# Four PSUM tiles in turn in place of three kept ones, and another order where pool mixer and output projection meet

## The chip, the cores and the metric

The kernel runs on one core of one Trainium2 chip. The number that counts is the device time in microseconds from the launch to the end of the last instruction; the median of three runs of the kernel before is 1367.88 us (1367.1 to 1373.0). The profiled execution, from which all rows below come, took 1365.11 us, with a span of 1363.2 us from its first to its last instruction. The five engines of the core are named PE (matrix multiply, with PEld for its weight loads), DVE (vector), ACT (scalar), POOL and SP; DMA queues move data between HBM and on-chip memory. Matrix products land in PSUM, which has eight banks of 512 fp32 numbers per partition; DVE or ACT must read a product out of its bank before PE may write there again.

## The reference

The program is one step of a streaming encoder for 1024 new frames of one stream and 32 of another (1056 columns of 1024 channels, all fp32), through two layers.

```
even:  h = rms_norm(x);  z = h @ w_in            # 5120 columns: a | u v | gate
       y_a = pool_mixer(a)                        # trailing means over 2/4/8/16 frames minus a, per-group 256x256 matrix, scale
       y_b = u * (W_s @ layer_norm(v) + b)        # per chunk of 128 frames, gelu(u), gelu(v); 4 head groups ("SGU")
       x = x + rms_norm((concat(y_a, y_b) * silu(gate)) @ w_out)
odd:   z = rms_norm(x) @ w_in                     # q latent | kv latent | rotary key | gate
       attention over latents, chunk-causal;  x = x + rms_norm((out * silu(gate)) @ w_o)
```

Outputs are both streams, the pool mixer's last 15 rows, v of the small stream and the caches of the odd layer.

## The kernel before

**Layout.** Channels lie on the partitions in blocks of 128, frames along the free axis. The 1056 frames are cut into an "a" group of 640 columns and a "b" group of 416. A product of fp32 accuracy is made of three matmuls, hi\*hi, hi\*lo and lo\*hi, on operands that have been split in two; the code names the halves `hi`/`lo`, `whi`/`wlo`. An output block of 128 channels over 8 input blocks takes, for the a group, 24 groups of two matmuls of 320 columns in a two-bank tile (`za`), and, for the b group, 24 matmuls of 416 columns in one bank (`zb`). `mm_block` issues them; "ab" interleaves both, "a" or "b" does one. `evac` and its like read the banks out.

**Stages.** In order of time (us from the span's start): the setup and a first part of the input projection; seven-product pairs of blocks (`pair_block`, to about 360); the *pool stage*, which projects the eight `a` blocks, forms the windowed means on DVE and POOL, and multiplies by the group matrices (`y_a`, about 360 to 476); the *junction*, where the last `y_a` and the first two blocks of the output projection meet (to about 510); the *first a loop*, the output projection's first half for m = 2 to 7, over pool channels; the *second a loop* for m = 0 to 7 over SGU channels (about 589 to 660), each followed by the addition to the first half and a running sum of squares (L828 to L832); the *b stage*, the same for the b columns (about 658 to 742, L842 to L860); then the odd layer, whose input projection runs to about 950. The spatial gating (SGU) is done meanwhile, one chunk of 128 frames at a time: four small groups of four matmuls into a bank tagged `mi`, each read by DVE at L764 and L765 into one of three scratch tiles `tm`, `dgh`, `dgl`.

**What sets the order.** PE runs in the order in which Python emits its instructions. A counter `self.now` adds up the cost of each matmul; at the end of each k step `poll` lets one waiting task go whose due time has come. A task yields the delay to its next step from the table `N`: `N["mixq"]` is the delay between the four `mi` groups of a chunk. Tasks can also be driven to an end ahead of their due times, as before `split_a` ("while len(done) < 5"), which needs five finished chunks. The other engines' order is set by the tile framework's scheduler from the dependencies; so are the semaphores, and a dependency holds for a whole tile, whichever part is written.

**PSUM.** The pool `ps` holds three two-bank tiles `zt` (z_9_80, z_10_81, z_11_82 in the rows below) and two one-bank `mi` tiles. After the pairs of blocks `zrot` deals them out: `za` goes in turn to z_10_81 and z_11_82, `zb` in turn to the two halves of z_9_80. In the junction `B2` is that same tile z_9_80, used as the `za` of the last `y_a`, whose `zb` goes to an `mi` bank; later B2 holds the squares of the second a loop. The squares of the b stage go to one of the other two.

`BOTH` names the blocks of the output projection whose first half is done for a and b together ("ab") in the first a loop, and copied out by `put`; the others' b columns get theirs in the b stage.

Of the kernel before, what the change touches and what calls it, by code (L numbers as in the profile page):

```python
# [10 lines left out]
F32 = mybir.dt.float32  # L11
F32R = mybir.dt.float32r
AF = mybir.ActivationFunctionType
ALU = mybir.AluOpType
AX = mybir.AxisListType
ET = mybir.EngineType
PSUM = bass.MemoryType.PSUM
DRAM = bass.MemoryType.DRAM

P = 128  # L20
# [3 lines left out]
NA, NB, CA = 640, 416, 320  # L24
# [7 lines left out]
        "kn e 2": 4.31, "v p 2": 5.302, "kn o 0": 6.344, "qn o 0": 6.796, "v p 3": 7.31, "v p 4": 8.3,  # L32
        "kn o 1": 8.827, "qn o 1": 10.546, "kn o 2": 12.035, "qn o 2": 12.785}

N = {"tp": 5500, "sa": 9000, "sl": 12000, "sb": 6000, "sbk": 2000, "sg": 500, "x": 462, "mix": 10626, "mixq": 1490, "tr": 717, "lead": 9500, "tr0": 11989, "res": 9194, "ra": 2699,
     "rb": 1574, "ha": 8000, "hb": 5000, "kv": 429, "q": 20908, "k": 34682, "kvs": 1773, "qs": 10662, "rest": 1357, "r1": 1608,
     "r2": 1337, "fa": 5400, "tn": 1800, "w0": 2000, "w1": 1552, "f0": 1645, "f1": 626, "fy": 648}
HF = 6
# [2 lines left out]
HT, HQ = 528, 264  # L41
RAW = 3
LO_POOL = ()
BOTH = (2, 3, 4, 5)
A_ORDER = [6, 7, 4, 5, 2, 3, 0, 1]
KS = 5
NV = 1184
# [25 lines left out]
def two(ap):  # L73
    return ap.rearrange("p (c n) -> p c n", c=2)


class Build:
    def __init__(self, ctx, tc, upto, aps):
        self.ctx, self.tc, self.nc = ctx, tc, tc.nc
        self.upto = upto  # L80
        for k, v in aps.items():
            setattr(self, k, v)
        self.uid = 0
        self.now = 0.0
        self.tasks = []
        self.rr = 0
        self.ca, self.nb = CA, NB
        self.banks = {}
        self.reps = {}
        self.zrot = None  # L90

# [32 lines left out]

    def bank(self, tag):

        if self.zrot and tag in ("za", "zb"):
            r = self.zrot[tag == "zb"]  # L130
            r.append(r.pop(0))
            return r[-1]
        tag, bufs = self.banks.get(tag, (tag, 2))
        return self.t(self.ps, [P, 2, 512] if tag in ("za", "sc") else [P, 512], F32, tag, bufs)

# [188 lines left out]
    def even(self):  # L324
        nc = self.nc
# [3 lines left out]
        L, R, ab, halves, evc = self.L, self.R, self.ab, self.halves, self.evc  # L329
# [68 lines left out]
        zt = self.zt  # L398
# [4 lines left out]
        for g in "ab":  # L403
            acc, *sqs = (v[:, mpos[g]] for v in sums)
            z = [(zt[0], None), (zt[1], None)] if g == "a" else [(None, zt[2][:, i, :]) for i in range(2)]
            for k in range(NK):
                x = split_x(g, k)
# [9 lines left out]
        pairs = [(10, 11), (34, 35), (36, 37), (12, 13), (14, 15), (38, 39)] + [(24 + 2 * i, 25 + 2 * i) for i in range(4)]  # L417
# [71 lines left out]
        for g, z in (("a", zz), ("b", z)):  # L489
# [3 lines left out]
            if g == "a":  # L493
                tp = self.spawn(t_prep(), N["tp"])
            for i in range(2):
                ps = (zt[i], None) if g == "a" else (None, zt[2][:, i, :])
# [40 lines left out]
        for p, (b0, b1) in enumerate(pairs):  # L537
# [18 lines left out]
            else:  # L556
                for e in range(2):
                    i = (b0, b1)[e] % 8
# [2 lines left out]
                        nc.vector.tensor_tensor(u, u, g, ALU.mult)  # L561
                        nc.scalar.dma_start(mBd[i], u)
        self.h2 = [(Pair(None, None), Pair(None, None)) for _ in range(NK)]
        zs = [zt[(7 * len(pairs) + i) % 3] for i in range(3)]
        self.zrot = [[zs[0], zs[2]], [zs[1][:, i, :] for i in range(2)]]


        self.shut(self.lb)
# [1 line left out]
        mix = {}  # L570
# [42 lines left out]
        def y_a(g, w, bank=None):  # L613

            wf = w[0]
            for m in range(2):
                c = [slice(k * 256 + m * P, k * 256 + (m + 1) * P) for k in range(2)]
                ps = self.mm_block(lambda k: (wf[0][:, c[k]], wf[1][:, c[k]]), dhl[g], range(2), ps=bank() if bank else None)
                blk = 2 * g + m
                gt, (pool, o) = gate[blk], mslot[blk]  # L620
                hi, lo = mix[blk] = tuple(ab(pool or self.rb, o + e, F32R) for e in range(2))
                nc.vector.scalar_tensor_tensor(two(gt.a), ps[0][:, :, :CA], self.vec(PSC, blk), two(gt.a), ALU.mult, ALU.mult)
                nc.vector.scalar_tensor_tensor(gt.b, ps[1][:, :NB], self.vec(PSC, blk), gt.b, ALU.mult, ALU.mult)
                for q in "ab":
                    nc.scalar.copy(hi.get(q), gt.get(q))  # L625
                    nc.vector.tensor_tensor(lo.get(q), gt.get(q), hi.get(q), ALU.subtract)
            del dhl[g]
            pfree.extend(held.pop(g))

        wp = {}  # L630
        for i, blk in enumerate(A_ORDER):
# [3 lines left out]
            else:  # L635
                wA = self.prep_w(self.i_wout[0, :, :1024])
            ps = self.mm_block(self.wcol(wts.pop(blk)), h, range(NK))
# [4 lines left out]
            a = pool_evac(blk, ps)  # L642
# [18 lines left out]
            if m in BOTH:  # L661
                nc.scalar.copy(yp[m].b, ps[1][:, :NB])  # L662

        part = {}
        for m in range(2):
            if m == 1:
                wA1 = self.prep_w(self.i_wout[1, :, :1024])
            part[m] = self.mm_block(self.wcol(wA if m == 0 else wA1), mix, A_ORDER[:6], "a", last=False)
        B2 = zs[1]
        y_a(pg, wp[pg], lambda: (B2, self.t(self.ps, [P, 512], F32, "mi")))  # L670
        for m in range(2):
            self.mm_block(self.wcol(wA if m == 0 else wA1), mix, A_ORDER[6:], "a", ps=part[m], first=False)
            put(m, part[m])
        wn = {2: self.prep_w(self.i_wout[2, :, :1024])}

# [143 lines left out]
        for m in range(NK):  # L819
            if m < 7:  # L820
                wn = self.prep_w(self.i_wout[m + 1, :, 1024:], lo_on=nc.vector)
            else:
                wA = self.prep_w(self.i_wout[6, :, :1024], lo_on=nc.vector)
            ps = self.mm_block(lambda k: self.wcol(wB)(k - 8), mix, range(8, 16), "a")
            if m < 7:
                wB = wn
            y = yp[m].a
            nc.vector.tensor_tensor(two(y), two(y), ps[0][:, :, :CA], ALU.add)  # L828
            sq = B2[:, :, :CA]
            nc.scalar.activation(two(acc) if m == 0 else sq, two(y), AF.Square)  # L830
            if m:
                nc.vector.tensor_tensor(two(acc), two(acc), sq, ALU.add)  # L832
        self.res = self.spawn(self.residual("a", acc, yp), N["res"])
        while len(done) < 9 or any(mix[8 + k][0].b is None for k in range(NK)):
            self.step(min((t for t in self.tasks if t is not self.res), key=lambda t: t[:2]))
        acc = ab(self.rb, 8, F32, "b").b
        za = self.zrot[0][0]
        order = [6, 7, 0, 1, 2, 3, 4, 5]
        jobs = [(m, c) for m in order for c in ((1,) if m in BOTH else (0, 1))]
        w = wA  # L840
        for j, (m, c) in enumerate(jobs):
            if j + 1 < len(jobs):  # L842
                mm, cc = jobs[j + 1]
                wn = self.prep_w(self.i_wout[mm, :, cc * 1024 : cc * 1024 + 1024], lo_on=nc.vector)
            if c == 0:
                ps = self.mm_block(self.wcol(w), mix, A_ORDER, "b", last=False)
                w = wn
                continue
            ps = None if m in BOTH else ps
            ps = self.mm_block(lambda k: self.wcol(w)(k - 8), mix, range(8, 16), "b", ps=ps, first=ps is None)  # L850
            w = wn
            y = yp[m].b
            if m in BOTH:
                nc.vector.tensor_tensor(y, y, ps[1][:, :NB], ALU.add)  # L854
            else:
                nc.vector.tensor_copy(y, ps[1][:, :NB])  # L856
            sq = za[:, m % 2, :NB]
            nc.scalar.activation(acc if m == order[0] else sq, y, AF.Square)
            if m != order[0]:
                nc.vector.tensor_tensor(acc, acc, sq, ALU.add)  # L860
# [50 lines left out]
    def odd_in(self):  # L911
# [110 lines left out]
        self.shut(self.evc)  # L1022
        self.shut(self.la)
        self.shut(self.ps)
        self.zrot = None


    def attention(self):
# [455 lines left out]
```

## Time and profile before

| what | value |
|---|---|
| median of three runs | 1367.88 us (1367.1 to 1373.0) |
| profiled execution | 1365.11 us, span 1363.2 us |
| busy | PE 1269.6 us (93%), DVE 860.6 (63%), ACT 552.2 (41%), POOL 306.0 (22%) |
| PE busy 360 to 476 | 101.90 of 116 us |
| PE busy 560 to 640 | 70.26 of 80 us |
| PE busy 640 to 750 | 92.77 of 110 us |
| PE busy 800 to 960 | 142.10 of 160 us |
| mean granted TensorE clock | 0.984 |

PE is busy nearly all the time, so what to read is what PE waits for when it is not. A row of the waits reads: the waiting engine, tile and line, the engine, tile and line that it waited for, and the time in all, the number of waits and the longest. In a timeline row stand the start, the length, the instruction, and in brackets the idle time before it with its releaser. All matmuls stand on L116, since one helper issues them: they are told apart by the names of their tiles.

### The profile page before, as it was taken

The page shows a single profiled execution, that of the slowest core. Times are in us where ns is not written, and L with a number is a line of the kernel's source. Part 1 is how long each engine was busy: PE and PEld are TensorE (multiplying, and loading weights), DVE is VectorE, ACT ScalarE, POOL GpSimd, SP SyncE. Part 2 cuts the span into 40 slices and gives each one's busy share as a digit, 9 for nine tenths or more (in the row PEclk, how much of TensorE's full clock was granted, in tenths as well). Part 3 has the DMA queues.
Part 4 walks back from the last instruction along what each step waited for, and adds up shares of the span by engine and source line. Part 5 has one row for each costly group of instructions (what it writes and reads, how often), then busy time and mean ns, then how long its engine had stood idle before and what let it go on. Part 6 is the DMA issues. An engine that isn't in the chain of part 4 may idle for free. (4 is left out here: it accounts for less than half of the span.)

```text
span 1363.2 us, 22025 instructions
## 1 busy us (share of the span) xinstructions
PE 1269.6 (93%) x8488; PEld 1228.1 (90%) x8488; DVE 860.6 (63%) x1613; ACT 552.2 (41%) x1027; POOL 306.0 (22%) x381
## 2 busy tenths in 40 slices
PE   9899999999988899989987989888999999999995
PEld 8899999999988899978886989888899999998994
DVE  7977776767576545698394833531766576665437
ACT  8634333334232222243242323322656565654431
POOL 0200000000232233534002353221322322222410
PEclk9999999999999999999998989989999999999998
DMA  6022223223323152222462332212111111116425
GB/s 218 32 71 87 87 86 112 102 70 105 118 73 117 50 198 86 85 80 76 129 219 82 105 123 91 98 57 87 33 46 52 46 48 50 41 48 196 152 85 193
DMA packets 75159, 130.73 MB, mean 96 GB/s; under 512 B 10448, under 2 KB 33424, under 8 KB 75056
## 3 DMA queue, kind: packets, MB, share of 16 engines
q1 hardware_dynamic: 56576, 101.24, 23.7%
q10 hardware_dynamic: 18480, 28.09, 5.6%
q8 instruction: 67, 1.10, 0.3%
q14 instruction: 36, 0.29, 0.1%
HBM read 97.42 MB, written 31.88 MB: 95 GB/s over the span
## 5 line engine op out<-in xcount | busy, mean ns | idle before, releaser
L116 PE MATMUL z<-l,whi 128*128 128x264 f32 (+2 forms) x2032 | 395.2, 308 | 31.8 <-DVE l L199 15.3
L116 PEld LDWEIGHTS z<-l,whi 128*128 128x128 f32 x2032 | 319.1, 191 | 39.5 <-DVE l L199 16.6
L116 PE MATMUL z<-l,wlo 128*128 128x264 f32 (+2 forms) x1240 | 269.0, 301 | 0.0
L155 ACT CAST whi<-raw 128x512 fp32r<-128x512 f32 (+1 forms) x180 | 108.1, 603 | 352.5 <-PE z L116 221.1
L156 POOL TENSOR_TENSOR wlo<-raw,whi 128x512 fp32r<-128x512 f32 (+2 forms) x122 | 155.6, 1277 | 348.2 <-ACT whi L155 344.0
L116 PEld LDWEIGHTS z<-l,wlo 128*128 128x128 f32 x1240 | 203.5, 191 | 0.3
L116 PE MATMUL z<-r,whi 128*128 128x264 f32 (+2 forms) x696 | 152.8, 307 | 15.6 <-DVE l L854 5.3
L116 PE MATMUL z<-a,whi 128*128 128x320 f32 x704 | 145.2, 312 | 1.5 <-ACT a L625 0.7
L116 PEld LDWEIGHTS z<-r,whi 128*128 128x128 f32 x696 | 114.5, 191 | 19.2 <-issue 4.8
L116 PEld LDWEIGHTS z<-a,whi 128*128 128x128 f32 x704 | 116.1, 188 | 2.9 <-ACT a L625 0.9
L1131 POOL TENSOR_SCALAR p<-p,nm 128x128 f32<-128x128 f32 (+8 forms) x72 | 53.0, 736 | 165.4 <-DVE nm L1130 130.1
L116 PE MATMUL z<-b,whi 128*128 128x416 f32 x240 | 77.4, 361 | 7.8 <-DVE l L856 2.8
L116 PE MATMUL z<-a,wlo 128*128 128x320 f32 x352 | 80.2, 309 | 0.0
L585 POOL MEMSET r<- 128x16 f32 x8 | 0.9, 112 | 310.4 <-PE mi L525 288.4
L448 ACT CAST whi<-r 128x512 fp32r<-128x512 f32 x56 | 34.8, 621 | 86.6 <-PE z L116 80.1
L1129 ACT ACTIVATE p<-sc,nm 128x128 f32<-128x128 f32 (+8 forms) x72 | 50.6, 703 | 44.7 <-DVE nm L1128 32.5
L116 PEld LDWEIGHTS z<-a,wlo 128*128 128x128 f32 x352 | 61.4, 188 | 0.2
L449 DVE TENSOR_TENSOR wlo<-r,whi 128x512 fp32r<-128x512 f32 x56 | 38.4, 686 | 36.0 <-ACT whi L448 35.9
L116 PE MATMUL sc<-a,whi 128*128 128x400 f32 x256 | 57.6, 346 | 0.2 <-ACT p L1129 0.2
L156 DVE TENSOR_TENSOR wlo<-raw,whi 128x512 fp32r<-128x512 f32 x58 | 39.7, 690 | 28.1 <-ACT whi L155 28.1
L1161 DVE TENSOR_TENSOR pl<-pj,ph 128x512 fp32r<-128x512 f32 (+2 forms) x96 | 51.1, 552 | 7.0 <-ACT ph L1160 6.3
L116 PEld LDWEIGHTS z<-b,whi 128*128 128x128 f32 x240 | 45.6, 192 | 10.3 <-ACT l L662 3.2
(305 smaller groups left out, 2634.4 us busy)
## 6 DMA issues: line engine op xcount, KB each, us to landing
raw<-in_w SPq DMA_DIRECT2D x64, 256.0 KB, 2.7
r<-in_w SPq DMA_DIRECT2D x56, 256.0 KB, 2.7
raw<-in_wout SPq DMA_DIRECT2D x56, 256.0 KB, 3.1
mBd<-r ACTq DMA_DIRECT2D x8, 528.0 KB, 2.7
gAd<-r ACTq DMA_DIRECT2D x8, 528.0 KB, 2.7
l<-mBd SPq DMA_DIRECT2D x8, 528.0 KB, 5.7
vd<-r ACTq DMA_DIRECT2D x16, 256.0 KB, 2.3
r<-vd SPq DMA_DIRECT2D x8, 512.0 KB, 3.6
```

The lines of the kernel that those rows point to most:

```text
L116: self.nc.tensor.matmul(out, lhsT, rhs, start=start, stop=stop)
L155: nc.scalar.copy(hi[:, :m], raw[:, :m])
L156: (lo_on or nc.gpsimd).tensor_tensor(lo[:, :m], raw[:, :m], hi[:, :m], ALU.subtract)
L448: nc.scalar.copy(hi, src)
L449: lo_on.tensor_tensor(lo, src, hi, ALU.subtract)
L585: nc.gpsimd.memset(a[:, 0:16], 0.0)
L1129: nc.scalar.activation(pv, view, AF.Exp, bias=nm[:n, 0:1], accum_out=nm[:n, 1:2])
L1131: nc.gpsimd.tensor_scalar(p[:n, :K], p[:n, :K], nm[:n, 2:3], 1.0, ALU.mult, ALU.mult)
L1161: nc.vector.tensor_tensor(lo[:, :nb, off : off + P], tr[:, :nb, :], hi[:, :nb, off : off + P], ALU.subtract)
```

## The change

After the pairs of blocks the pool `ps` is closed, and a pool `psb` with two tiles for each tag is opened in its place: `za` twice (two banks each), `zb` twice, `mi` twice, again eight banks. `zrot` and `B2` go. In the junction the first block of the output projection is done for a and b together over six of eight input blocks, the last `y_a` follows with tiles of its own, then the second block, and then the rest of both. `BOTH` is (0, 3, 4, 5) in place of (2, 3, 4, 5), so that block 0 has its b columns early and block 2 late, and the b stage goes through the blocks in the order 6, 7, 1, 2, 0, 3, 4, 5. The squares of the second a loop are made in two halves of 320 columns in `zb` banks, and those of the b stage in a `za` tile. `N["mixq"]` goes from 1490 to 2600.

```diff
-... "mix": 10626, "mixq": 1490, "tr": 717, ...
+... "mix": 10626, "mixq": 2600, "tr": 717, ...
-BOTH = (2, 3, 4, 5)
+BOTH = (0, 3, 4, 5)
     def bank(self, tag):
-        if self.zrot and tag in ("za", "zb"):
-            r = self.zrot[tag == "zb"]
-            r.append(r.pop(0))
-            return r[-1]
         tag, bufs = self.banks.get(tag, (tag, 2))
         return self.t(self.ps, [P, 2, 512] if tag in ("za", "sc") else [P, 512], F32, tag, bufs)
...
-        zs = [zt[(7 * len(pairs) + i) % 3] for i in range(3)]
-        self.zrot = [[zs[0], zs[2]], [zs[1][:, i, :] for i in range(2)]]
+        self.shut(self.ps)
+        self.ps = self.open("psb", bufs=2, space=PSUM)
...
-        part = {}
-        for m in range(2):
-            if m == 1:
-                wA1 = self.prep_w(self.i_wout[1, :, :1024])
-            part[m] = self.mm_block(self.wcol(wA if m == 0 else wA1), mix, A_ORDER[:6], "a", last=False)
-        B2 = zs[1]
-        y_a(pg, wp[pg], lambda: (B2, self.t(self.ps, [P, 512], F32, "mi")))
-        for m in range(2):
-            self.mm_block(self.wcol(wA if m == 0 else wA1), mix, A_ORDER[6:], "a", ps=part[m], first=False)
+        part = {0: self.mm_block(self.wcol(wA), mix, A_ORDER[:6], "ab", last=False)}
+        wA1 = self.prep_w(self.i_wout[1, :, :1024])
+        y_a(pg, wp[pg])
+        part[1] = self.mm_block(self.wcol(wA1), mix, A_ORDER[:6], "a", last=False)
+        for m, w in ((0, wA), (1, wA1)):
+            self.mm_block(self.wcol(w), mix, A_ORDER[6:], "a" if m else "ab", ps=part[m], first=False)
             put(m, part[m])
...
-            sq = B2[:, :, :CA]
-            nc.scalar.activation(two(acc) if m == 0 else sq, two(y), AF.Square)
-            if m:
-                nc.vector.tensor_tensor(two(acc), two(acc), sq, ALU.add)
+            for c in range(2):
+                yc, ac = two(y)[:, c], two(acc)[:, c]
+                sq = ac if m == 0 else self.bank("zb")[:, :CA]
+                nc.scalar.activation(sq, yc, AF.Square)
+                if m:
+                    nc.vector.tensor_tensor(ac, ac, sq, ALU.add)
...
-        za = self.zrot[0][0]
-        order = [6, 7, 0, 1, 2, 3, 4, 5]
+        order = [6, 7, 1, 2] + list(BOTH)
...
-            sq = za[:, m % 2, :NB]
+            sq = self.bank("za")[:, 0, :NB]
...
-        self.zrot = None
```

PE issues as many matmuls as before. At three places the rows show what moved. In a row stand the position in the engine's order, the line (the changed file is a few lines shorter), the operation, the written tile and the read ones, and the size.

The first place is PE in the pool stage, where one `y_a` block ends and the next begins (`whi` is a group matrix, the `r` are the two halves of the windowed means). Before:

```order
1610 L116 MATMUL z_9_80<-r_419_4211,whi_4225 128x416
1611 L116 MATMUL z_10_81<-r_418_4210,wlo_4226 128x320 x2
1612 L116 MATMUL z_9_80<-r_418_4210,wlo_4226 128x416
1613 L116 MATMUL z_11_82<-r_400_4067,whi_4225 128x320 x2
1614 L116 MATMUL z_9_80<-r_400_4067,whi_4225 128x416
1615 L116 MATMUL z_11_82<-r_401_4068,whi_4225 128x320 x2
```

and in the changed kernel:

```order
1610 L115 MATMUL zb_4331<-r_423_4219,whi_4233 128x416
1611 L115 MATMUL za_4330<-r_422_4218,wlo_4234 128x320 x2
1612 L115 MATMUL zb_4331<-r_422_4218,wlo_4234 128x416
1613 L115 MATMUL za_4360<-r_402_4073,whi_4233 128x320 x2
1614 L115 MATMUL zb_4361<-r_402_4073,whi_4233 128x416
1615 L115 MATMUL za_4360<-r_403_4074,whi_4233 128x320 x2
```

The order is the same; the two blocks' b columns went to one tile, z_9_80, and now go to two, zb_4331 and zb_4361.

The second place is PE in the junction, around the start of the last `y_a` (rows with `whi_5125`, `whi_4993` or `whi_5183` and their `wlo` are output projection, those with `whi_5074` or `whi_5106` the last `y_a`). Before, after 36 matmuls each for blocks 0 and 1:

```order
1946 L116 MATMUL z_10_81<-a_512_4938,whi_5125 128x320 x2
1947 L116 MATMUL z_10_81<-a_514_4940,whi_5125 128x320 x2
1948 L116 MATMUL z_10_81<-a_512_4938,wlo_5126 128x320 x2
1949 L116 MATMUL z_9_80<-r_517_4954,whi_5074 128x320 x2
1950 L116 MATMUL mi_5172<-r_517_4954,whi_5074 128x416
1951 L116 MATMUL z_9_80<-r_518_4955,whi_5074 128x320 x2
```

and in the changed kernel, after 54 matmuls for block 0 alone; the second piece is the end of `y_a` and the start of block 1:

```order
1946 L115 MATMUL zb_5121<-b_541_4971,whi_4993 128x416
1947 L115 MATMUL za_5120<-a_538_4968,wlo_4994 128x320 x2
1948 L115 MATMUL zb_5121<-b_539_4969,wlo_4994 128x416
1949 L115 MATMUL za_5188<-r_543_4984,whi_5106 128x320 x2
1950 L115 MATMUL zb_5189<-r_543_4984,whi_5106 128x416
1951 L115 MATMUL za_5188<-r_544_4985,whi_5106 128x320 x2
```

```order
1970 L115 MATMUL zb_5219<-r_555_5090,whi_5106 128x416
1971 L115 MATMUL za_5218<-r_555_5090,wlo_5107 128x320 x2
1972 L115 MATMUL zb_5219<-r_555_5090,wlo_5107 128x416
1973 L115 MATMUL za_5248<-a_440_4350,whi_5183 128x320 x2
1974 L115 MATMUL za_5248<-a_442_4352,whi_5183 128x320 x2
```

The last `y_a` thus stands between the two partial blocks where it stood behind both, with 54 matmuls ahead of it instead of 72.

The third place is DVE where the chunks are driven to the fifth before `split_a`, at the seam of the two a loops. L764/L765 read the `mi` banks (L756/L757 in the changed kernel), L787 (L779) is `split_a`, L729, L734 and L745 (L721, L726, L737) prepare a chunk. Before:

```order
622 L729 BN_STATS bs_6181<-r_680_6039 128x6
623 L765 SCALAR_TENSOR_TENSOR tm_6088<-mi_6071,vecs_69,tm_6088 128x128
624 L764 SCALAR_TENSOR_TENSOR dgh_6101<-mi_6095,vecs_69,r_577_5296 128x128
625 L156 TENSOR_TENSOR wlo_6145<-raw_6143,whi_6144 128x512
626 L765 SCALAR_TENSOR_TENSOR dgh_6101<-mi_6095,vecs_69,dgh_6101 128x128
627 L764 SCALAR_TENSOR_TENSOR dgh_6101<-mi_6095,vecs_69,r_577_5296 128x128
628 L764 SCALAR_TENSOR_TENSOR dgl_6113<-mi_6108,vecs_69,r_577_5296 128x128
```

and in the changed kernel:

```order
623 L757 SCALAR_TENSOR_TENSOR tm_6135<-mi_6129,vecs_69,tm_6135 128x128
624 L756 SCALAR_TENSOR_TENSOR dgh_6166<-mi_6142,vecs_69,r_610_5358 128x128
625 L779 TENSOR_TENSOR a_448_4382<-l_600_5332,a_446_4380 128x640
626 L721 BN_STATS bs_6149<-r_717_6054 128x6 x2
627 L757 SCALAR_TENSOR_TENSOR dgh_6166<-mi_6142,vecs_69,dgh_6166 128x128
628 L723 BN_AGGR sm_6152<-bs_6149 128x2
629 L756 SCALAR_TENSOR_TENSOR dgh_6166<-mi_6142,vecs_69,r_610_5358 128x128
630 L724 TENSOR_SCALAR sm_6152<-sm_6152 128x1
631 L779 TENSOR_TENSOR a_489_4650<-l_601_5333,a_487_4648 128x640
632 L726 TENSOR_SCALAR r_717_6054<-r_717_6054,sm_6152 128x1024
633 L757 SCALAR_TENSOR_TENSOR dgh_6166<-mi_6142,vecs_69,dgh_6166 128x128
```

On PE, two `mi` groups (mi_6095, mi_6108) stood directly behind one another here, and now four do (mi_6129, mi_6142, mi_6161, mi_6173), with no other matmul between them. Behind this place, in the second a loop, 12 or 24 matmuls of 320 columns stand between one group and the next before, and 6 to 24, mostly 18 or 24, after.

More of the change, by code (lines that the diff above doesn't have):

```diff
@@ L33 @@
         "kn o 1": 8.827, "qn o 1": 10.546, "kn o 2": 12.035, "qn o 2": 12.785}
-N = {"tp": 5500, "sa": 9000, "sl": 12000, "sb": 6000, "sbk": 2000, "sg": 500, "x": 462, "mix": 10626, "mixq": 1490, "tr": 717, "lead": 9500, "tr0": 11989, "res": 9194, "ra": 2699,
+N = {"tp": 5500, "sa": 9000, "sl": 12000, "sb": 6000, "sbk": 2000, "sg": 500, "x": 462, "mix": 10626, "mixq": 2600, "tr": 717, "lead": 9500, "tr0": 11989, "res": 9194, "ra": 2699,
      "rb": 1574, "ha": 8000, "hb": 5000, "kv": 429, "q": 20908, "k": 34682, "kvs": 1773, "qs": 10662, "rest": 1357, "r1": 1608,
@@ L1024, in odd_in @@
         self.shut(self.ps)
-        self.zrot = None
     def attention(self):
```

## The prediction

> **What bounds the kernel now.** I read the page first, then the waits of PE stage by stage, then single gaps in the timeline.
>
> ```profile
> PE 1269.6 (93%) x8488; PEld 1228.1 (90%) x8488; DVE 860.6 (63%) x1613; ACT 552.2 (41%) x1027; POOL 306.0 (22%) x381
> ```
>
> PE is busy for 93%. The change leaves its matmuls as they are, so it can only alter the 94 us of the 1363.2 us span in which PE is not busy, and the clock. The waits of PE by stage (pool stage 360 to 476, junction and first blocks 476 to 560, seam and second a loop 560 to 640, b stage 640 to 750, odd projection 800 to 960):
>
> ```profile
> PE z L116 <- DVE r L589: 7.1, 7, 1.2
> PE z L116 <- DVE b L623: 4.9, 4, 1.6
> PE z L116 <- DVE r L623: 2.1, 2, 1.1
> ...
> PE z L116 <- ACT l L662: 2.5, 3, 1.5
> PE z L116 <- DVE a L622: 0.8, 1, 0.8
> PE z L116 <- ACT a L625: 0.7, 1, 0.7
> PE z L116 <- DVE a L626: 0.3, 1, 0.3
> ...
> PE mi L116 <- DVE tm L765: 4.6, 2, 2.9
> PE mi L116 <- DVE dgh L765: 2.4, 2, 1.3
> PE mi L116 <- DVE dgl L765: 2.1, 2, 1.5
> ...
> PE z L116 <- DVE l L856: 5.9, 4, 3.1
> PE z L116 <- DVE l L854: 5.3, 3, 3.7
> PE z L116 <- DVE b L860: 3.6, 1, 3.6
> PE z L116 <- DVE rep L832: 2.5, 1, 2.5
> ...
> PE z L116 <- DVE l L199: 15.3, 9, 5.6
> ```
>
> Nearly all are waits of a z tile on DVE, and the lines waited for (L589, L623, L662, L199, L854, L856) are the last to read the b columns of the block just before. Whether the other half of the same tile is free does not help: PE stops at each seam until that read is done. Three seams of the pool stage in the timeline of PE:
>
> ```profile
> 419.23 0.94 PE L116 MATMUL z<-l,whi 128*128 128x416 f32 x4 [0.99 <-DVE r L589]
> 432.10 0.94 PE L116 MATMUL z<-r,whi 128*128 128x416 f32 x4 [1.00 <-DVE r L589]
> 436.31 0.94 PE L116 MATMUL z<-r,whi 128*128 128x416 f32 x4 [1.05 <-DVE b L623]
> ```
>
> **Pool stage: 14.1 us there (7.1 + 4.9 + 2.1), 13.4 taken away.** With two `zb` tiles a block waits for the read two blocks back. A full block lasts 432.10 - 419.23 - 1.00 = 11.9 us and a `y_a` block 436.31 - 432.10 - 1.05 = 3.2 us. What must be done within the shorter one is:
>
> ```profile
> L587 DVE TENSOR_TENSOR r<-z,rep 128x640 f32<-128x640 f32 x7 | 5.8, 825 | 37.8 <-PE z L116 37.8
> L588 DVE TENSOR_TENSOR r<-z,rep 128x384 f32<-128x384 f32 x7 | 3.8, 548 | 0.0
> L622 DVE SCALAR_TENSOR_TENSOR a<-z,vecs,a 128x640 f32<-128x640 f32 x4 | 3.5, 880 | 0.2 <-PE z L116 0.2
> L623 DVE SCALAR_TENSOR_TENSOR b<-z,vecs,b 128x416 f32<-128x416 f32 x4 | 2.6, 641 | 0.0
> ```
>
> 0.83 + 0.55 us or 0.88 + 0.64 us of DVE against 3.2 us, so 1.6 us are to spare for another instruction ahead of it. I leave 0.7 us for a seam where two come together. If that cover were gone, all 14.1 us would stay.
>
> **Junction: 1.8 us there (0.8 + 0.7 + 0.3), 0.3 added.** The last `y_a` comes 18 matmuls of 320 columns earlier, but its b columns now find their place in a new tile. The second `y_a` block needs the first `za` of two, held by part 0, so it must wait for the first's L622 and L623, and the block behind it for the second's L622: 0.8, some 0.5 and 0.8 us, the first by its row, the others by L622 and L623. Bounds: 1.8 saved, 1.5 lost. The first blocks of the output projection wait 2.5 us for ACT's L662, the copy of the block before out of the shared tile; two `zb` tiles are enough for all 2.5 to go. Bounds: 0 and 2.5. Block 1's weights are still loaded behind part 0's matmuls, on SP's queue in the same order, and are needed two `y_a` blocks (6.4 us) later than before; block 0 has its b columns from weights that are there anyway, and block 2 loads its own again in the b stage, as block 0 did. No DMA is added, and I cost this at nothing.
>
> **SGU: 4.0 us taken away, 4.4 added.** The three mi rows are 9.1 us: one wait of 2.9 at the seam and five between.
>
> ```profile
> 588.94 0.65 PE L116 MATMUL mi<-r,r 128*128 128x256 f32 x4 [2.91 <-DVE tm L765]
> 592.22 0.56 PE L116 MATMUL z<-a,whi 128*128 128x320 f32 x2 [0.53 <-DVE a L787]
> ...
> L745 DVE TENSOR_TENSOR r<-r,r 128x1024 fp32r<-128x1024 f32 (+1 forms) x6 | 7.4, 1238 | 0.3 <-ACT r L735 0.3
> L729 DVE BATCH_NORM_STATS2 bs<-r 128x6 f32<-128x512 f32 (+1 forms) x10 | 6.7, 683 | 2.6 <-DMA r<-vd 2.6
> L765 DVE SCALAR_TENSOR_TENSOR dgl<-mi,vecs,dgl 128x128 f32<-128x128 f32 x17 | 5.9, 345 | 0.2
> L787 DVE TENSOR_TENSOR a<-l,a 128x640 fp32r<-128x640 f32 x7 | 5.6, 849 | 0.0
> L734 DVE TENSOR_SCALAR r<-r,sm 128x1024 f32<-128x1024 f32 (+1 forms) x5 | 4.3, 858 | 4.2 <-POOL sm L733 4.2
> L832 DVE TENSOR_TENSOR rep<-rep,z 128x640 f32<-128x640 f32 x3 | 2.4, 815 | 0.0
> ```
>
> The wider delay puts 18 or 24 matmuls between groups of the second a loop where 12 stood; the five waits add up to 9.1 - 2.9 = 6.2 us, and I take 4.0 of them as gone, with bounds of 0 and 6.2. At the seam four groups stand together where two stood. The last one may not start before mi_6142 is read; from the end of the read of mi_6129 DVE has, by the rows of its order, four L764/L765 (0.34 each), two L787 (0.85 each), two L729 (0.68 each), L734 (0.86) and small ones: 1.4 + 1.7 + 1.4 + 0.9 = 5.4 us. Of that about 0.6 us is the third group's own PE time, and successive DVE instructions overlap by some 0.4 in all: 4.4 us. The second and third wait about 2.4 and 1.0 us, in the same way (L745 with 1.24 stands before one). So 7.8 us against 2.9 + 0.5 before: 4.4 added. DVE does part of `split_a` meanwhile, which the block behind needs anyhow, so as little as 0 may be added; with POOL's answer ahead of L734 (4.2 us idle over five) up to 5.3.
>
> Halving the squares makes seven L832 into fourteen of 320 columns: by the 384-column L588 at most 0.55 us each, where half of 0.82 stood, so 0 to 14 x 0.55 - 7 x 0.82 = 2.0 us more on DVE, and some such on ACT, which is busy 41%. Both lie beside the matmuls of eight blocks. If DVE had no room at all it would cost those 2.0 us; I take nothing.
>
> **b stage: 9.5 us taken away.**
>
> ```profile
> 709.75 0.62 PE L116 MATMUL z<-r,whi 128*128 128x416 f32 x2 [3.06 <-DVE l L856]
> 719.80 0.43 PE L116 MATMUL z<-r,whi 128*128 128x416 f32 x1 [3.72 <-DVE l L854]
> 741.90 1.43 PE L116 MATMUL z<-l,whi 128*128 128x320 f32 x4 [3.56 <-DVE b L860]
> ...
> 700.00:720.00 20.00, 13.22 (x61) 12.35 (x60) 18.36 (x27) 10.34 (x17) 0.00 (x0) 0.91 0.74 250
> ```
>
> L856 and L854 are 11.2 us in all. The two long ones (3.06 + 3.72 = 6.8) fall where DVE is busy 18.36 of 20 us (the number behind the length, PE and PEld) and the DMA engines 0.74: there the residual of the a columns runs on DVE, which also splits the weights of each block. A second tile lets PE go on, and then it meets the weights. I take 2.5 of the 6.8, bounds 0 and 6.8. The other five, 4.4 us, are single reads of 0.6 us like those of the pool stage: all go. L832's 2.5 is the last square before the b stage, which still must be read before its bank is free; I leave it. L860's 3.6 is the first odd block, waiting for the tile that held the squares: a block now takes the tile of the square before the last. 2.6 of it goes, bounds 0 and 3.6. The residual of the b columns follows PE's own order behind this, so it starts earlier with PE.
>
> **Odd projection: 14.8 of 15.3 us taken away.** Each of its nine waits is for the b read of the block before; a block has the matmuls of the full one above (11.9 us) and more between them, and the longest wait is 5.6, where DVE was late. Double tiles give a whole block. Bounds: 9.7, should the long one stay, and 15.3.
>
> **Granted clock: 4.0 us taken away.** In 4-us windows (second last but one number, the granted clock, before DMA share and GB/s):
>
> ```profile
> 740.00:744.00 4.00, 2.10 (x8) 2.10 (x9) 1.84 (x5) 0.52 (x1) 0.88 (x1) 0.68 0.19 66
> 856.00:860.00 4.00, 2.91 (x11) 2.88 (x12) 1.52 (x5) 2.62 (x4) 0.93 (x1) 0.68 0.68 188
> 892.00:896.00 4.00, 3.71 (x13) 3.65 (x14) 0.23 (x1) 0.94 (x2) 0.00 (x0) 0.50 0.35 135
> 896.00:900.00 4.00, 4.00 (x20) 3.95 (x20) 0.00 (x0) 0.00 (x0) 0.00 (x0) 0.70 0.00 0
> 588.00:592.00 4.00, 2.74 (x18) 2.51 (x18) 4.00 (x11) 2.69 (x4) 2.15 (x5) 1.00 0.17 49
> ```
>
> Behind some long waits the clock falls for one or two windows: 4 x 0.32 = 1.3 us of matmul time lost at 741, 1.3 at 857, 4 x (0.50 + 0.30) = 3.2 at 892, but nothing behind the 2.9 at 588.94. Without those three waits 5.8 us come back; a seam of 4.4 us may cost 1.3 of them again. I take 4.0, with bounds of 0 and, for the waits at 709 and 719 at 1.3 to 3.2 each besides, 10. [...]
>
> **The sum.** 1365.1 (profiled execution) - 13.4 + 0.3 - 2.5 - 4.0 + 4.4 - 9.5 - 14.8 - 4.0 = 1321.6. The median before is 1367.9, 2.8 more than the profiled execution, so on its scale the forecast is **1324 us**, 3.2% faster. Its own range, with the small bounds only, is 1316 to 1333.
>
> **The rivals.**
>
> *DVE and the weights take over.* A wait on a tile may hide a wait for what is behind it: DVE's work and DMA stay as large. For it speak the 18.36 of 20 us above; against it, DVE idle in the pool stage (L587 waited 37.8 us for PE) and DVE's 63% overall. Then the b stage gives nothing (9.5), the clock half (2), the odd projection keeps its late read (5): 1324 + 16.5 = 1340 us.
>
> *All of it goes.* The bounds on the far side: two more in the SGU, 4.4 at the seam saved by `split_a` being done there, 4.3 + 1 in the b stage, 6 of clock: 1324 - 18 = 1306 us.
>
> *The seams of the SGU pay it back (slower).* Nine chunks have 36 groups. Six of them wait 9.1 us now, 1.5 each. If the interleaving of two chunks that the wider delay brings made each of the 36 wait like those six, that would be 36 x 1.52 - 9.1 = 45.6 us more, and without the SGU terms (+0.4 net) the sum is 1323.7: 1369 us, slower from 1.5 us a group on. For it: the seam shows 2.9 us for two groups in a row; against: between groups of the second a loop there is more PE work than before.
>
> *The separate tiles are no cure.* If the reads were waited for because DVE is also the one that PE hears from last, and not because of the tile, the waits stay: 1368 us. Against it: the waits name just the reader of that tile, and L587 and L622 show DVE waiting for PE before the read, not PE for a late DVE.
>
> **How the numbers follow.** Chances: forecast 0.50, DVE takes over 0.27, all of it 0.13, SGU 0.05, no cure 0.05. The range, 8 in 10, goes from 1312, inside the second rival, to 1344, past the first. Faster by over 0.5% (about 7 us, what a measurement can tell from none) is 0.90; within it 0.06; slower 0.04.
>
> **What would show it.** In the changed kernel the waits of z on the reads of `pool_evac`, `y_a` (L622, L623), `put` and of the odd evacuation (L199) should be under 1 us a stage, and the pool stage without gaps of 1 us between blocks. At the seam there should be a wait of over 3 us for a mi bank. In the b stage a long wait should name weights or wlo rather than a z read. Wrong would be: z waits that stay (no cure), or mi waits of over 20 us (SGU). If waits vanish and the time doesn't, DMA or DVE starved PE elsewhere.

## The result, and the profile after

The changed kernel takes 1316.8 us in the median against 1367.5 us of the kernel before in the same runs; the ratio is 0.962, with a 95% interval of 0.9585 to 0.9658. Run once more beside other kernels it gave 0.9625 (0.9606 to 0.9644). One execution in which the clock was low throughout (0.84) is left out. The forecast was 1324 us, so 43.5 us of gain were foretold and 50.7 came.

The page of the changed kernel, its busy times:

```profile
span 1315.4 us, 22052 instructions
PE 1261.1 (96%) x8488; PEld 1227.6 (93%) x8488; DVE 865.7 (66%) x1620; ACT 552.2 (42%) x1035; POOL 304.3 (23%) x381
```

PE's time without work fell from 93.6 to 54.3 us, and its busy time from 1269.6 to 1261.1 us, with the same 8488 matmuls. Together that is the 47.8 us between the spans. The waits of PE in the changed kernel from the pool stage to the end of the odd projection (engine, tile, line waited for; time in all, number, longest):

```profile
PE mi L115 <- DVE dgh L757: 7.9, 2, 5.2
PE mi L209 <- DVE r L900: 5.2, 1, 5.2
PE mi L115 <- DVE dgl L757: 4.2, 2, 2.6
PE mi L115 <- DVE tm L757: 2.5, 2, 1.7
PE mi L115 <- DVE dgh L227: 2.0, 1, 2.0
PE zb L115 <- DVE rep L826: 1.9, 1, 1.9
PE sc L115 <- DVE knl L1050: 1.4, 1, 1.4
PE mi L115 <- DVE dgl L227: 1.0, 1, 1.0
PE za L115 <- DVE r L617: 0.9, 1, 0.9
PE zb L115 <- DVE l L847: 0.8, 2, 0.5
PE za L115 <- DVE a L617: 0.8, 1, 0.8
PE zb L115 <- ACT whi L150: 0.7, 1, 0.7
...
```

Not one wait for the evacuation of the block just before is left in the pool stage and in the odd projection. The z waits that remain are the two of the junction (L617), one before the b stage (L826), and three short ones in it. The mi waits of the SGU (L757) have grown, from 9.1 to 14.6 us, and two new waits have come (L227, 3.0 us). L227 makes two diagonal matrices from the inverse roots of the a columns' sums of squares, and PE multiplies with them to spread that scale over the partitions; both waits stand just behind the first matmuls of the odd layer.

By stage, in us of PE's waits, before and after:

| where | before | after | forecast of the difference | measured |
|---|---|---|---|---|
| pool stage | 14.1 | 0 | -13.4 | -14.1 |
| junction | 1.8 | 1.7 | +0.3 | -0.1 |
| first blocks (L662) | 2.5 | 0 | -2.5 | -2.5 |
| SGU, between blocks | 6.2 | 5.9 | -4.0 | -0.3 |
| SGU, seam (with L787) | 3.4 | 8.8 | +4.4 | +5.4 |
| b stage, z | 17.3 | 3.4 | -9.5 | -13.9 |
| b stage, L227 | 0 | 3.0 | none | +3.0 |
| odd projection, pj with it | 16.7 | 0 | -14.8 | -16.7 |

### The profile page after: what moved, and what is told of

Its sections match the earlier page's. It is cut to its first block, busy times and chain, and to the rows that moved or that the text cites. A ratio compares the mean times of both kernels' runs of the same rounds, so it can differ in the third digit from the quotient of the medians.

```text
span 1315.4 us, 22052 instructions
## 1 busy us (share of the span) xinstructions
PE 1261.1 (96%) x8488; PEld 1227.6 (93%) x8488; DVE 865.7 (66%) x1620; ACT 552.2 (42%) x1035; POOL 304.3 (23%) x381
## 4 chain that ended last, share of the span: by engine, by line
PE 82%; DVE 9%; issue 3%; DMA 2%; ACT 1%; POOL 1%; SPq 0%; ACTq 0%; DVEq 0%; POOLq 0%
PE z L115 24%; PE za L115 18%; PE zb L115 12%; PE sc L115 12%; PE pj L115 11%; PE pj L1150 2%; PE mi L115 1%; DVE wlo L151 1%; PE mi L209 1%; PE mi L520 1%; DMA r<-vd 1%; DVE r L900 1%; DVE a L1373 1%; DMA rawa<-ogd 0%; DVE a L1374 0%
## 5 line engine op out<-in xcount | busy, mean ns | idle before, releaser
L115 PE MATMUL z<-l,whi 128*128 128x264 f32 (+2 forms) x1312 | 245.3, 292 | 5.3 <-DVE r L192 2.1
L150 ACT CAST whi<-raw 128x512 fp32r<-128x512 f32 (+1 forms) x180 | 108.0, 603 | 306.5 <-PE zb L115 117.1
L115 PEld LDWEIGHTS z<-l,whi 128*128 128x128 f32 x1312 | 195.0, 189 | 7.9 <-ACT r L377 2.4
L115 PE MATMUL z<-l,wlo 128*128 128x264 f32 (+2 forms) x880 | 185.9, 290 | 0.0
L115 PE MATMUL za<-a,whi 128*128 128x320 f32 x704 | 147.1, 317 | 0.9 <-DVE r L617 0.9
L115 PEld LDWEIGHTS za<-a,whi 128*128 128x128 f32 x704 | 119.2, 193 | 1.6 <-ACT whi L150 1.2
L115 PE MATMUL za<-l,whi 128*128 128x320 f32 (+1 forms) x496 | 112.6, 317 | 0.0
L115 PEld LDWEIGHTS za<-l,whi 128*128 128x128 f32 x496 | 90.5, 191 | 0.7
L115 PE MATMUL z<-r,whi 128*128 128x264 f32 x448 | 90.6, 284 | 0.0
L115 PE MATMUL za<-a,wlo 128*128 128x320 f32 x352 | 81.6, 313 | 0.0
L115 PE MATMUL zb<-l,whi 128*128 128x416 f32 x224 | 76.4, 353 | 0.0
```

Of the source, the lines that this page charges most:

```text
L115: self.nc.tensor.matmul(out, lhsT, rhs, start=start, stop=stop)
L150: nc.scalar.copy(hi[:, :m], raw[:, :m])
```

## Is it the tiles? Two halves of one tile again

```diff
+        zbt = self.t(self.ps, [P, 2, 512], F32, "zbt", 1)
+        self.zh = [zbt[:, i, :] for i in range(2)]
...
     def bank(self, tag):
+        if self.zh and tag == "zb":
+            self.zh.append(self.zh.pop(0))
+            return self.zh[-1]
...
+        kept = self.zh.pop()
         y_a(pg, wp[pg])
+        self.zh.append(kept)
```

This is the changed kernel with the two `zb` banks as halves of one tile, in turn (the half that block 0 holds is kept out of the last `y_a`). There are eight banks again, and the order of the program is the same.

> The changed kernel with one edit: the two zb banks are again the two halves of one two-bank tile, in turn; junction, order, delay and squares stay as changed. If the waits of the kernel before came from the sharing of one tile (theory): about 14 us of z waits return in the pool stage, 2.5 behind it, 8 to 14 in the b stage, 13 to 17 in the odd projection, and 4 to 8 of granted clock: 1350 to 1366 us. If the order at the junction, the delay or the split squares brought the gain (rival): under 1325 us.

Measured: 1372.6 us, ratio to the kernel before 1.0019 (1.0003 to 1.0035). All the gain is gone, and the time is above the 1350 to 1366 us that the tile was expected to give. Its waits of PE over the same stretch:

```profile
PE zbt L116 <- DVE l L198: 15.1, 9, 5.6
PE zbt L116 <- DVE r L590: 8.1, 8, 1.2
PE zbt L116 <- DVE l L857: 6.8, 4, 4.0
PE mi L116 <- DVE dgh L765: 6.4, 2, 4.7
...
PE zbt L116 <- DVE b L624: 4.9, 4, 1.6
PE zbt L116 <- DVE l L855: 4.6, 3, 3.0
PE mi L116 <- DVE dgl L765: 4.0, 2, 2.5
PE zbt L116 <- DVE rep L834: 2.9, 1, 2.9
PE mi L116 <- DVE tm L765: 2.4, 2, 1.9
PE zbt L116 <- DVE r L624: 2.1, 2, 1.1
PE pj L116 <- DVE l L198: 1.4, 1, 1.4
...
```

The waits for the read of the block before are back, nearly with their old sums: 15.1 us in 9 in the odd projection (15.3 in 9 before), 4.9 and 2.1 after the `y_a` blocks (the same), 8.1 on L590 (7.1 in the pool stage as before, and 1.0 at the first block of the output projection), 6.8 and 4.6 in the b stage (5.9 and 5.3). Only L860's 3.6 us, which was a wait for a `za` tile, stays away, and L662's (now L663) is 0.9 in place of 2.5. The two banks are different banks in both kernels, and the matmul never writes what is being read. So the wait belongs to the dependency, which is kept for a whole tile. The junction's order, the delay and the halved squares are all in this run, and it is not faster than the kernel before: the rival that they had brought the gain is out. Whether the separate tiles would give all of it without the new order at the junction and the halved squares, no run shows.

That this run is slower than expected is the clock's doing. PE's time without work is 92.8 us (93.6 before), but its busy time is 1277.8 us (1269.6), at a mean granted clock of 0.973 in the profiled execution (0.984). It has the old waits and the SGU's longer ones too; some of its falls of the clock stand where no wait was altered (0.51 in the 4-us window at 36 us, where 0.78 stood before, and 0.65 in that at 64 us, where 1.00 stood), and why it has those stays open.

## What the other edits are worth

**The order of blocks.**

```diff
-BOTH = (0, 3, 4, 5)
+BOTH = (2, 3, 4, 5)
...
-        part = {0: self.mm_block(self.wcol(wA), mix, A_ORDER[:6], "ab", last=False)}
+        part = {0: self.mm_block(self.wcol(wA), mix, A_ORDER[:6], "a", last=False)}
...
-        order = [6, 7, 1, 2] + list(BOTH)
+        order = [6, 7, 0, 1] + list(BOTH)
```

> The changed kernel with BOTH back at (2, 3, 4, 5), block 0 done for the a columns alone at the junction, b stage in the order 6, 7, 0, 1, 2, 3, 4, 5. If that edit is worth nothing by itself: 1315 to 1318 us, with z waits at the junction still 1.0 to 1.8 us; the last y_a then has 36 matmuls ahead of it, 5.3 us, so if the means feeding it are late by then, a new wait of up to 3 us on ACT or DVE stands before it, and 1318 to 1321.

Measured: ratio 0.9639 (0.9616 to 0.9661), the median 1319.1 us. No new wait stands before the last `y_a`: its two waits are again for L617, 0.8 us each. Its mi waits are 13.8 us, as long as in the changed kernel. By itself the edit is worth nothing that can be told.

**The delay between groups.**

```diff
-"mixq": 2600
+"mixq": 1490
```

> The changed kernel with the delay between a chunk's four groups back at 1490, so that three groups in place of four stand in a row at the seam, and 12 or 24 matmuls between groups of the second a loop. If the two halves of the delay edit cancel as the forecast has it (4.0 gained between the blocks, 4.4 lost at the seam): the seam's waits fall from 8.8 us to about 6, the waits in the second a loop go from 2.6 to about 4.5, and the time stays within 2 us of the changed kernel's 1316.8. If the wider delay is a plain loss: 1310 to 1312. If it is a gain of its own: 1320 or more.

Measured: ratio 0.9589 (0.9568 to 0.961), 1312.6 us. Its SGU waits:

```profile
PE mi L115 <- DVE tm L757: 4.1, 4, 1.2
PE mi L115 <- DVE dgl L757: 2.8, 2, 1.7
PE mi L115 <- DVE dgh L757: 2.1, 2, 1.1
PE mi L115 <- ACT r L727: 1.6, 1, 1.6
```

10.6 us in place of 14.6, in nine waits in place of six, none over 1.7. The waits between the blocks are 6.2 by the timeline, as much as before the change, and those of the seam 4.4. In these rounds the kernel before took 1369.9 us; on the scale of the 1316.8 us the ratio gives 1311.3, inside the 1310 to 1312 expected if the wider delay is a plain loss. The interval overlaps that of the changed kernel, so the loss is likely rather than shown by this run alone.

**Both undone.** The two diffs above together leave the four tiles, the order at the junction and the halved squares.

> The changed kernel with both edits of tables undone (BOTH and the b stage's order as before, delay 1490); what is left is the four tiles, the order at the junction and the halved squares. PE's groups then stand at the seam as before, two in a row. If the four groups in a row are the price of the table edits (theory): SGU waits of 9 to 11 us in place of 14.7, no wait over 3.2 us at the seam, and 4 to 7 us less than the changed kernel. If the SGU's waits are just DVE's work (rival): 13 us or more of them, within 2 us of the changed kernel.

Measured: ratio 0.9582 (0.9564 to 0.96), 1311.5 us, where the changed kernel itself took 1317.5 us beside it at 0.9625 (0.9606 to 0.9644).

> The changed kernel once more, so that it stands beside the others on one chip: a ratio to the kernel before of 0.960 to 0.965 (all theories).

The intervals do not touch: the two edits of tables cost some 6 us. The runs with one of them undone put most of that on the delay (0.9589) and none on `BOTH` (0.9639). The mi waits, and where the longest stands:

```profile
PE mi L115 <- DVE tm L757: 4.3, 2, 2.9
PE mi L115 <- DVE dgh L757: 2.6, 2, 1.3
PE mi L115 <- DVE dgl L757: 2.2, 2, 1.6
...
569.79 0.65 PE L115 MATMUL mi<-r,r 128*128 128x256 f32 x4 [2.91 <-DVE tm L757]
```

9.1 us, the same six waits as in the kernel before, to the tenth in sum, with the seam's at 2.9. With the tables of before, the SGU is as it was, and the rest of the gain is untouched.

**An earlier start of each chunk.** If the four groups in a row are the trouble, chunks that start closer together should help:

```diff
-"lead": 9500
+"lead": 8000
```

> The changed kernel with the delay between the starts of two chunks at 8000 in place of 9500, so that two groups stand in a row at the seam in place of four. If the seam's 8.8 us of waits are the price of the four groups: they fall to about 3.5 and the time to 1310 to 1313. If DVE is full around the seam whatever the order, and the waits are only its backlog: they come back elsewhere between 510 and 650, and the time stays within 2 us of 1316.8.

Measured: ratio 0.9652 (0.9632 to 0.9672), 1320.8 us, not faster. Two groups stand in a row at the seam now, but:

```profile
552.82 0.64 PE L115 MATMUL mi<-r,r 128*128 128x256 f32 x4 [3.32 <-DVE dgl L757]
...
577.33 0.90 PE L115 MATMUL mi<-r,r 128*128 128x256 f32 x4 [4.77 <-DVE dgh L757]
...
605.90 1.09 PE L115 MATMUL mi<-r,r 128*128 128x256 f32 x4 [4.31 <-DVE tm L757]
```

17.0 us of mi waits, before, at and behind the seam. That groups which come closer on the whole only meet the same DVE work sooner is a reading of these rows; no run isolates it.

**DVE's load.** To tell whether DVE's work as such is too much, POOL takes over the low halves of the second a loop's weights, 16 subtractions of 0.7 us:

```diff
-                wn = self.prep_w(self.i_wout[m + 1, :, 1024:], lo_on=nc.vector)
+                wn = self.prep_w(self.i_wout[m + 1, :, 1024:])
             else:
-                wA = self.prep_w(self.i_wout[6, :, :1024], lo_on=nc.vector)
+                wA = self.prep_w(self.i_wout[6, :, :1024])
```

once with the delay 1490, once as changed (2600), and once with both tables undone:

> The changed kernel with the delay at 1490 and, in the second a loop, the low halves of the weights made by POOL in place of DVE (16 of them, 0.7 us each on DVE by the row of L156, some 1.28 on POOL). If the mi waits of the SGU are DVE's backlog (theory): they fall from the 10.6 us of the run with 1490 alone to 3 to 6, and the time to 1304 to 1309 on the scale on which that run took 1312.6. If they come from the order in which groups and chunks stand (rival): they stay at 9 us or more and the time at 1311 to 1314. If POOL is then late with weights: a new z wait on POOL's wlo, and no gain.

> The changed kernel, delay 2600 kept, with the low halves of the second a loop's weights made by POOL in place of DVE. If the seam's 8.8 us are DVE's backlog: about 4 to 6 there, the 2.6 at 625 gone, and 1310 to 1313 us on the scale on which the changed kernel took 1316.8. If they are set by the four groups in a row, each of which must be read before the next but one may start: 8 us or more at the seam still.

> The last kernel with the low halves of the second a loop's weights on POOL. If DVE's load adds to the SGU's waits: 2 to 4 us less of them and of time than without. If not: within 1 us.

Measured: 0.9573 (0.955 to 0.9597) where the same without was 0.9589; 0.9608 (0.958 to 0.9635) where the changed kernel was 0.9621; 0.9599 (0.9579 to 0.9618) where the same without was 0.9582. None of the three can be told from its own base, and with 1490 the mi waits are far from the 3 to 6 us of a mere backlog. The mi waits fell from 10.6 to 8.9, from 14.6 to 11.8, and rose from 9.1 to 11.0. With 2600 the wait at 625 went, but the seam kept its waits:

```profile
568.41 1.09 PE L115 MATMUL mi<-r,r 128*128 128x256 f32 x4 [2.98 <-DVE dgh L757]
570.36 1.09 PE L115 MATMUL mi<-r,r 128*128 128x256 f32 x4 [0.85 <-DVE tm L757]
576.60 1.09 PE L115 MATMUL mi<-r,r 128*128 128x256 f32 x4 [5.16 <-DVE dgh L757]
```

For the seam these runs decide little. Only one of the 16 subtractions stands ahead of it in the changed kernel (561.19, 0.64 us; the next starts at 577.00, behind the last wait), so POOL took hardly any DVE work away there. With the delay 1490 two stand in it (566.33 and 569.97, 1.6 us together), and without them its waits are 4.6 us in place of 4.4. What does speak on the seam is the kernel with both tables undone:

```profile
PE 1256.8 (96%) x8488; PEld 1223.2 (94%) x8488; DVE 864.5 (66%) x1620; ACT 552.8 (42%) x1035; POOL 307.8 (24%) x381
```

DVE has nearly the same work in all (864.5 us, 865.7 in the changed kernel), and the seam's waits are 2.9 and not 8.8. So the seam is a matter of what stands ahead in DVE's order rather than of DVE's total; whether fewer instructions just ahead of it would help the changed kernel was not tried. What stands there, in the changed kernel, from the end of the second wait to the start of the last:

```profile
570.44 0.34 DVE L756 SCALAR_TENSOR_TENSOR dgh<-mi,vecs,r 128x128 f32<-128x128 f32 x1
571.36 0.82 DVE L779 TENSOR_TENSOR a<-l,a 128x640 fp32r<-128x640 f32 x1 [0.58 <-ACT a L778]
572.11 1.28 DVE L721 BATCH_NORM_STATS2 bs<-r 128x6 f32<-128x512 f32 x2
573.30 0.33 DVE L757 SCALAR_TENSOR_TENSOR dgh<-mi,vecs,dgh 128x128 f32<-128x128 f32 x1
...
573.94 0.91 DVE L779 TENSOR_TENSOR a<-l,a 128x640 fp32r<-128x640 f32 x1
575.28 0.81 DVE L726 TENSOR_SCALAR r<-r,sm 128x1024 f32<-128x1024 f32 x1 [0.43 <-POOL sm L725]
576.01 0.35 DVE L757 SCALAR_TENSOR_TENSOR dgh<-mi,vecs,dgh 128x128 f32<-128x128 f32 x1
```

The four reads of mi_6142, with 1.4 us of work of their own, are spread over 5.9 us (570.44 to 576.36) by two instructions of `split_a`, the statistics of the next chunk and its scaling, which waits for POOL. That is the list on which the forecast's 4.4 us were worked out; it measured 5.2.

**A wait that the change left.** L900 adds up seven squares at the end of the b columns' residual, and PE waits for it 5.3 us before (L907 there) and 5.2 after. On top of the kernel with 1490 and POOL's low halves:

```diff
-                sqs.append(sq)
+                if m:
+                    nc.gpsimd.tensor_tensor(acc2, acc2, sq, ALU.add)
...
-        for sq in sqs[1:]:
-            nc.vector.tensor_tensor(acc2, acc2, sq, ALU.add)
```

> The kernel with delay 1490 and the low halves on POOL (e5), in which POOL also adds up the squares of the b columns' residual, one after each block, in place of seven adds on DVE at the end. The wait of 5.2 us on L900, which the change left as it was, is DVE's backlog if DVE was busy without a break before it: then it falls to 0 to 3 us and the time by 2 to 5. If POOL's adds are slower than DVE's (its rows show 1.3 us where DVE takes 0.7) and come last: 4 us or more of wait, on L214's sum by POOL, and no gain.

Measured: 0.9588 (0.9565 to 0.9611) against 0.9573 without: no gain. The wait is gone and two others have taken its place, 2.1 us for high halves of weights from ACT and 1.8 for low halves, which POOL makes behind its adds, as the timelines of PE and POOL show:

```profile
754.38 0.85 PE L115 MATMUL za<-l,whi 128*128 128x320 f32 x4 [2.10 <-ACT whi L150]
757.06 0.90 PE L115 MATMUL za<-l,wlo 128*128 128x320 f32 x2 [1.83 <-POOL wlo L151]
...
752.98 2.45 POOL L898 TENSOR_TENSOR r<-r,r 128x416 f32<-128x416 f32 x2 [2.58 <-ACT r L896]
755.39 4.07 POOL L151 TENSOR_TENSOR wlo<-raw,whi 128x512 fp32r<-128x512 f32 x3
```

Of the versions tried, 1490 with or without BOTH undone and with or without POOL's low halves lie at 0.957 to 0.960 and cannot be told from each other; all of them beat the kernel before, and the one with both tables undone beats the changed kernel beside it.

## Why the prediction was right, and where its terms were not

**The pool stage, L662 and the odd projection** went as worked out: the cover of one block was enough everywhere, the late read of 5.6 us included. The forecast left 0.7 and 0.5 us for seams that come together, and nothing stayed. It had not counted the wait of 1.4 us for the last read of the odd projection (tile pj), which went too.

**The junction** stayed what it was, 1.7 us in two waits on the first and the second L622 (now L617); the third one forecast, for the b read, did not show.

**The b stage** was undersized. The step that failed is "a second tile lets PE go on, and then it meets the weights": of the 6.8 us in the two long waits, 2.5 were taken as gone, and all were. The weights cost 0.7 us (L150), once, where 3.72 had stood. DVE's 18.36 of 20 us was read as a bound. But PE had stood still there for the very reads that DVE did late; in the changed kernel DVE is busy 25.24 of the 26 us from 680 to 706, and PE waits 1.6 us there. So with a block's more room nearly the same DVE work fits. The single reads did not all go as forecast: two on L847 keep 0.8 us together.

The first odd block's 3.6 us went whole, but 3.0 came back a few matmuls later, on L227, for which the forecast had no term. Before, PE stood still at the first odd block while the scale of the a columns was made. Now it comes there sooner, and the scale is made later: POOL takes the inverse root (L217) at 713.16, behind two low halves of weights that end at 713.20, though DVE had the sums ready at 710.18. In the kernel before, POOL took it 0.1 us behind DVE.

**The SGU** was the other way round. The seam's term was right in place and mechanism, 8.8 us for a forecast 7.8. The 4.0 us expected from the wider delay did not come: 0.3 did. The bounds given were 0 and 6.2, and the value chosen was on the wrong end of them. The wider delay lets two chunks run at once, and their groups fall 6 or 12 matmuls apart in places; the wait at 624.87 (2.6 us) is such a place. With the low halves on POOL the groups stand just as close there and that wait is gone, so DVE's load has its part in it. The rival in which each of the 36 groups waits did not happen; the waits were six, as before.

**The clock** term failed, and another one that was not in the sum took its place. 4.0 us were to come back from the granted clock. Those behind the waits at 709 to 744, 857 and 892 did (8.5 us), but the seam's wait of 5.2 (2.7 us; its lines below) and the waits at 625 (1.5), 716 (1.4) and 904 (2.9) lost as much:

```profile
576.00:580.00 4.00, 3.50 (x14) 3.53 (x15) 3.87 (x7) 1.68 (x2) 0.97 (x1) 0.50 0.16 42
580.00:584.00 4.00, 4.00 (x24) 4.00 (x23) 3.70 (x10) 2.08 (x3) 1.34 (x3) 0.80 0.55 154
```

Summed over 4-us windows of the whole span, PE's busy time times the part of the clock not granted was 14.0 us before and 13.0 after. With both tables undone it is 8.5, at a mean clock of 0.988, and with the halves of one tile 23.5. The profiled executions with and without the tables' edits are 9.6 us apart (1315.4 and 1305.8): 5.5 are mi waits (14.6 and 9.1) and most of the rest is this clock, 4.5. Only 1.2 of the 4.5 stand at the seam and 1.5 behind the wait at 625. The largest, 2.9 at 904, stands behind the waits with which the attention begins, and nearly the same waits cost nothing with the tables undone (the last section); 1.5 at 64 us go the other way.

PE's busy time fell by 8.5 us all the same. The 7.5 that are not clock are, by an estimate from these rows, the price of stopping. Two groups of matmuls, six groups apart, in a block of the changed kernel:

```profile
416.17 0.46 PE L115 MATMUL za<-l,whi 128*128 128x320 f32 x2
...
419.07 0.46 PE L115 MATMUL za<-l,whi 128*128 128x320 f32 x2
```

2.90 us, without a stop. A `y_a` block of six such groups in the kernel before took 4.21 us from seam to seam, of which 1.05 were shown as waiting: 3.16, so a stop costs 0.26 us beside its idle time. All six such blocks give 0.22 to 0.27. The lists of PE's waits count 61 stops over the whole span before and 31 after; 30 times 0.25 are the 7.5. The sum of the forecast took the idle time alone. The rival "all of it goes" (1306 us) was the nearer in the z waits; the seam, the SGU and the clock kept the time from it.

**The total.** PE's waits in the table fell by 39.1 us, where their terms add up to 39.5. That this agrees is luck: the b stage gave 4.4 us more than its term, the pool stage, the junction and the odd projection 3.0 more, and the SGU 4.7 and L227 3.0 less. The clock then gave 3.0 less than foretold, and the stops 7.5 that had no term. So 47.6 us came between the profiled executions (1365.1 and 1317.5) where 43.5 were foretold. The mechanism, the shared tile, was right; the nearness of the number rests in part on errors that cancel.

## What to carry to other kernels

Where a dependency is kept for a whole tile, two buffers that are halves of one tile are one buffer: a row that shows the first matmul of each block waiting for the last read of the block before, while the other half is free, was cured here by two tiles in place of the halves (a ratio of 0.962 with the tiles, 1.0019 with the halves). Count a stop of PE as its idle time and, in this kernel, some 0.25 us more (the estimate above), and look behind each long one for the granted clock (0.50 behind the seam's 5.2 us, 1.00 behind the 2.91 us of the kernel before). A change of tables that comes with such a cure is best measured without it: here the kernel without the tables' edits had all of the gain, and the tables took 6 us back.

## What was not expected of the hardware

A wait of 2.91 us left the clock at 1.00 at the seam of the kernel before, and behind a wait of the same 2.91 us at the same place with both tables undone it was 0.83 and 0.74:

```profile
568.00:572.00 4.00, 2.21 (x12) 2.24 (x13) 4.00 (x13) 2.06 (x4) 1.53 (x4) 0.83 0.03 8
572.00:576.00 4.00, 4.00 (x23) 4.00 (x22) 4.00 (x8) 3.10 (x5) 2.32 (x3) 0.74 0.19 57
```

So the length of a wait alone did not decide here. Nor did a fall take a wait of that length. Where the attention begins, the changed kernel waits 0.69 and 1.35 us with one matmul between (904 to 906), and the clock is 0.50 in the window behind (first line). With both tables undone the waits there are 0.57, 1.36 and 0.26 us (897 to 900), and the clock stays at 1.00 (second line). A wait of 1.96 us that ends near 60.5 us, ahead of all that the change touches, keeps 1.00 in the kernels before and after, and with both tables undone the clock is 0.76 behind it (third line):

```profile
908.00:912.00 4.00, 4.00 (x13) 4.00 (x13) 1.13 (x4) 2.11 (x4) 0.37 (x1) 0.50 0.00 0
...
900.00:904.00 4.00, 3.86 (x24) 3.86 (x25) 1.82 (x7) 2.73 (x6) 0.38 (x1) 1.00 0.00 0
...
60.00:64.00 4.00, 3.37 (x13) 3.26 (x14) 3.97 (x8) 2.12 (x4) 0.00 (x0) 0.76 0.09 29
```

The clock fell behind one wait of 2.91 us and behind two shorter ones with a matmul between them, and stayed at 1.00 behind waits of the same or nearly the same lengths. What decides between them, no run here shows.
